# One score chunk of an attention kernel moved from ScalarE to VectorE, with joined norm exponentials and a new order of work

## The chip, the core and the metric

The kernel runs on one core of one Trainium2 chip. The metric is device time in microseconds (us), the median of several runs; smaller is better. Engines go by the profile's short names: PE is TensorE (matmuls), PEld its loading of weights, ACT is ScalarE, DVE is VectorE, POOL is GpSimd and SP the engine that issues most transfers.

## The reference

Attention on normalised vectors: 8 batches of 12 heads, 512 positions, 64 dimensions, tau = 0.1.

```python
def reference(Q, K, V, tau):                        # each (8, 12, 512, 64), float32
    Q_norm = Q / (norm(Q, axis=-1) + 1e-10)
    K_norm = K / (norm(K, axis=-1) + 1e-10)
    scores = einsum('bhqd,bhkd->bhqk', Q_norm, K_norm) / tau
    weights = exp(scores - max(scores))
    weights = weights / (sum(weights) + 1e-10)
    return einsum('bhqk,bhkd->bhqd', weights, V)
```

## The kernel before

Two heads of one batch make a pair; there are 48 pairs, 0 to 47. Every piece of work is an operation with a key, and the text speaks of it by that key: `SCO.24.1` is the score matmuls of pair 24, chunk 1. The operations of a pair s are:

- `LD.s.0`, `LD.s.1`, `LV.s` (SP): load Q, K and V of the pair, 256 KB each. Rings of 18 buffers for Q and K and 6 for V: `LV.s` waits until `VC.(s-6)` has read the buffer.
- `SQ.s` (POOL): squares of Q and K. `SSQ.s` (PE) and `RED.s` (DVE) sum them; `NEW.g.k` (DVE) are the Newton steps that turn the sums of a group g of up to two pairs into 1/norm. Steps 7 and, where one pair of the group is scaled on another engine than the other, 8, write the factors of K.
- `SCL.s.0` (DVE) and `SCL.s.1` (POOL, or DVE where the table `ON` says so): Q and K times 1/norm, as bf16.
- `TR.s` (PE) and `EVA.s` (DVE): transpose them and copy the transposes out of PSUM.
- `SCO.s.c` (PE), c from 0 to 3: a chunk of 128 keys against 512 queries for both heads, two matmuls into one of two halves of the score tile `sc_ps` (line 526). `EXP.s.c` (ACT, line 542): the exponential of 128x1024 scores, written as bf16 to `et`. The two halves alternate, so the SCO of a chunk waits for the EXP two chunks before it.
- `PV.s.h.t` (PE, line 570): `et` times V, with a column of ones that gives the sum of the weights; `RCP.s` and `NRM.s` (DVE) divide by it; `ST.s` (SP) stores. `et` has three buffers: `EXP.s` waits for the last PV of pair s-3.
- `VC.s` (POOL): V as bf16.

Pairs 0 to 2 (the head) take their 1/norm from ScalarE: `LN` and `EX` (line 286). There `EX.1.0` and `EX.1.1`, and `EX.2.0` and `EX.2.1`, are one for Q and one for K. Pair 0 is cut in halves by head (`LD.0.w.h`, `SQ.0.w.h`, `SCL.0.w.h`, `TR.0.w.h`, `EVA.0.w.h`, with w 0 for Q and 1 for K).

PSUM has a bank `n_ps` for the norms: sums, Newton steps and, in the head, factors lie in its first 272 columns. VectorE works in it with RED, NEW and SCL.

What sets the order: `ORDER` holds for each engine the list of its operations, written out by hand or by a planner outside of the file, and each engine does its list in that order. A wait of one operation holds back all that stands behind it on its engine. `schedule()` adds the waits for shared PSUM banks; `run()` turns every need into a semaphore.

A path for exponentials on VectorE is in the file but unused, since `SPLIT` is empty: `split()` (line 593) scores one head of a chunk into bank `x` (operation SCD), with a second matmul that adds a constant to lift the scores to the place where their bits are nearly those of a bf16 exponential, and four VectorE steps (EXD) then put a cubic correction on the low 16 bits and write the result as 16-bit integers.

The functions that the change touches, and what calls them:

## Time and profile before

| | before |
|---|---|
| median of 3 runs | 191.02 us |
| lowest and highest | 190.3 and 191.06 us |
| span of the profiled execution | 189.4 us |
| its own device time | not listed apart from the three |
| granted TensorE clock | 0.996 |
| exponentials of 128x1024 (line 542) | 184, 169.1 us busy |
| ScalarE busy | 181.7 us, 96% |
| TensorE, VectorE, GpSimd busy | 174.1, 148.1, 160.7 us |

The span runs from the first to the last instruction of one profiled execution; the device time has what lies around it as well. A busy time is the union of an engine's instructions, so where one starts before the one ahead of it has ended, the count times the mean is more than the busy time. In a row of the timeline stand the start, the duration, the engine, the line, what is written and read, and how many instructions were merged; in square brackets, the idle time of the engine before it and what ended that. A row of windows has the busy time of each engine in one stretch.

### The profile page before, as it was taken

What the parts mean: (1) busy time and instruction counts of PE and PEld (TensorE: products, weight loads), DVE (VectorE), ACT (ScalarE), POOL (GpSimd) and SP (SyncE); (2) the same over time, 40 slices, a digit from 0 to 9 for tenths busy, and PEclk for the clock granted to TensorE, in tenths of its full rate; (3) what the DMA queues carried; (4) which work ended last, traced back from release to release, by engine and by line L of the source; (5) the groups of instructions that cost most, each with busy time, mean ns of one, the idle gap of its engine ahead of it and who ended that gap; (6) DMA issues with size and microseconds to landing.
All of it is one profiled execution on the core that took longest, in us unless ns stands there. A gap on an engine that the chain in (4) does not pass through costs nothing.

```text
span 189.4 us, 7341 instructions
## 1 busy us (share of the span) xinstructions
PE 174.1 (92%) x3078; PEld 110.7 (58%) x3078; DVE 148.1 (78%) x453; ACT 181.7 (96%) x210; POOL 160.7 (85%) x147
## 2 busy tenths in 40 slices
...
GB/s 169 338 352 349 350 350 349 350 376 383 151 197 356 291 345 315 269 376 323 359 361 378 271 167 336 257 332 345 328 160 313 168 12 9 211 177 140 141 107 173
DMA packets 52448, 50.80 MB, mean 268 GB/s; under 512 B 3136, under 2 KB 52416, under 8 KB 52416
## 3 DMA queue, kind: packets, MB, share of 16 engines
...
q8 instruction: 24, 0.39, 0.9%
q10 hardware_dynamic: 432, 0.33, 0.6%
...
## 4 chain that ended last, share of the span: by engine, by line
ACT 82%; DVE 7%; PE 7%; DMA 1%; issue 1%
ACT et L542 80%; PE scps L526 2%; DMA qk<-in_Q_dram 1%; DVE qn L296 1%; PE bps L570 1%; DVE ob L586 1%; DVE qt L504 1%; ACT et L371 1%; PE bps L339 1%; PE bps L558 1%; DVE nps L276 1%; PE bps L268 1%; DVE ob L643 1%; PE bps L498 0%; DVE xs L324 0%
## 5 line engine op out<-in xcount | busy, mean ns | idle before, releaser
L542 ACT ACTIVATE et<-scps 128x1024 bf16<-128x1024 f32 x184 | 169.1, 1128 | 0.5 <-PE scps L526 0.4
L250 POOL TENSOR_TENSOR sq<-qk 128x1024 bf16<-128x1024 f32 (+2 forms) x48 | 87.9, 1848 | 5.1 <-DMA qk<-in_Q_dram 4.9
L526 PE MATMUL scps<-qt 64*128 64x512 bf16 x376 | 74.4, 385 | 8.4 <-ACT et L542 6.1
L570 PEld LDWEIGHTS bps<-vb,et 128*128 128x128 bf16 x1472 | 51.4, 98 | 24.1 <-issue 18.0
L570 PE MATMUL bps<-vb,et 128*128 128x65 bf16 x1472 | 65.1, 194 | 0.2
L296 POOL TENSOR_TENSOR qn<-qk,rk 128x512 bf16<-128x512 f32 x44 | 45.8, 1051 | 11.8 <-DVE rk L405 11.7
L504 DVE COPY qt<-bps 128x1024 bf16<-128x1024 bf16 x46 | 31.8, 691 | 10.1 <-PE bps L498 9.4
L296 DVE TENSOR_TENSOR qn<-qk,nps 128x512 bf16<-128x512 f32 (+1 forms) x51 | 33.9, 671 | 0.8 <-ACT nps L286 0.2
L586 DVE TENSOR_TENSOR ob<-bps,rd 128x512 f32<-128x512 f32 x47 | 32.5, 691 | 1.2
L526 PEld LDWEIGHTS scps<-qt 64*128 64x128 bf16 x376 | 18.2, 93 | 25.3 <-ACT et L542 13.4
L547 POOL TENSOR_SCALAR vb<-vf 128x512 bf16<-128x512 f32 x48 | 29.9, 634 | 0.0
L268 PE MATMUL bps<-sq,ident 128*128 128x128 bf16 x376 | 29.1, 220 | 0.0
L268 PEld LDWEIGHTS bps<-sq,ident 128*128 128x128 bf16 x376 | 21.2, 98 | 9.4 <-issue 6.3
L584 DVE RECIPROCAL rd<-bps 128x8 f32<-128x8 f32 x47 | 9.7, 207 | 17.7 <-PE bps L570 14.3
L498 PE MATMUL bps<-ident,qn 64*128 64x64 bf16 x736 | 18.8, 191 | 2.4 <-DVE ob L586 0.4
L498 PEld LDWEIGHTS bps<-ident,qn 64*128 64x128 bf16 x736 | 14.2, 95 | 9.8 <-DVE nps L276 4.0
L276 DVE TENSOR_REDUCE nps<-bps 128x16 f32<-128x128 f32 x45 | 13.4, 297 | 1.8 <-PE bps L268 1.8
L397 DVE TENSOR_TENSOR nps<-nps,ys 128x32 f32<-128x32 f32 (+1 forms) x48 | 9.2, 193 | 0.9
L401 DVE SCALAR_TENSOR_TENSOR nps<-nps,ys 128x32 f32<-128x32 f32 (+1 forms) x48 | 9.1, 191 | 0.8
L237 PE MATMUL scps<-warm_in 128*128 128x256 bf16 x22 | 4.8, 402 | 1.1 <-DVE warm_in L232 1.1
L409 DVE TENSOR_SCALAR ys<-nps 128x32 int32<-128x32 int32 (+1 forms) x24 | 4.4, 183 | 0.5
L405 DVE SCALAR_TENSOR_TENSOR nps<-nps,ys 128x16 f32<-128x16 f32 (+1 forms) x25 | 4.3, 175 | 0.3
...
## 6 DMA issues: line engine op xcount, KB each, us to landing
vf<-in_V_dram SPq DMA_DIRECT2D x48, 256.0 KB, 5.4
qk<-in_Q_dram SPq DMA_DIRECT2D x47, 256.0 KB, 5.9
qk<-in_K_dram SPq DMA_DIRECT2D x47, 256.0 KB, 5.7
out_dram<-ob SPq DMA_DIRECT2D x47, 256.0 KB, 4.4
...
```

The source lines that it names most:

```text
L250: emit = lambda e: e.tensor_tensor(out=b, in0=a, in1=a, op=ALU.mult)
L268: last = e.matmul(out=ps[:, 0:128], lhsT=ident[:, :], rhs=sq[s % R_SQ][:, :, 8 * k : 8 * k + 8], start=(k == 0), stop=(k == 7))
L276: lambda e: e.tensor_reduce(out=dst(None), in_=ps[:, 0:128].rearrange("p (w g e) -> p w g e", w=2, e=8), axis=AX.X, op=ALU.add))
L296: lambda e: e.tensor_tensor(out=o, in0=x, in1=r, op=ALU.mult))
L498: last = e.transpose(t_ps[:, k, b, :], qn[s % R_QN][ks, b // NT, b % NT].rearrange("p h d -> p (h d)"), ident[ks, ks])
L504: lambda e, lo=lo, hi=hi: e.tensor_copy(out=qt[iqt][:, :].rearrange("p w t (k x) -> p k (w t) x", k=2)[:, :, lo:hi], in_=t_ps[:, :, lo:hi]))
L526: last = e.matmul(out=sc_ps[:, 2 * b + k, :], lhsT=qt[iqt][64 * h : 64 * h + 64, 1, n, :], rhs=qt[iqt][64 * h : 64 * h + 64, 0, :, :], sta ...
L542: lambda e, c=c, b=b: e.activation(out=et[iet][:, c, :, :], in_=sc_ps[:, 2 * b : 2 * b + 2, :], func=ACT.Exp, scale=scale, bias=bias))
L547: lambda e: e.tensor_scalar(out=vb[:, iq, :, :, 0:DIM].rearrange("p c h d -> p h c d"), in0=vf[iv][:, :, :].rearrange("p h (c d) -> p h c ...
L570: last = e.matmul(out=o_ps[:, h, 65 * t : 65 * t + 65], lhsT=et[iet][:, c, h, 128 * t : 128 * t + 128], rhs=vb[:, iq, c, h, :], start=(c = ...
L584: lambda e: e.reciprocal(out=rd[io][:, :], in_=grid[:, :, :, DIM]))
L586: lambda e: e.tensor_tensor(out=ob[io][:, :], in0=grid[:, :, :, 0:DIM], in1=rd[io][:, :].unsqueeze(3).to_broadcast([128, 2, NT, DIM]), op= ...
```

## The change

- `SPLIT` names chunk 1 of pair 24. `SCO.24.1` and `EXP.24.1` go. For each head h and half j of the queries there is a `SCD.24.h.j` (PE: two matmuls of 256 columns) and four steps `EXD.24.h.j.0` to `.3` (DVE, 128x256). `split()` no longer scores 512 columns into bank `x` but 256 into the second half of the norm bank.
- Since PE then writes into a bank that VectorE uses all the time, `schedule()` makes each SCD wait for the last RED, NEW, SCL or EXD that stands on VectorE ahead of that SCD's first EXD. Each SCD also waits for the last EXD of the one before.
- The other three exponentials of pair 24 get the bias `SHIFT`, which makes them fit the shifted scale.
- For pairs 1 and 2 one EX does Q and K at once, so `EX.1.1` and `EX.2.1` go.
- `SCL.12.1` and `SCL.18.1` go from POOL to DVE; each splits a group's factors of K, so that `NEW.6.8` and `NEW.9.8` come in.
- Two memsets (`level0`, `level`) fill the constant's tile on DVE at the start.
- The order of all five engines is new. What else it moves that matters here: `LD.1.1` goes second on SP; `SQ.1.1.1` and `SQ.1.0` go ahead on ACT; `SQ.1.1.0` goes ahead of the EVA of pair 0 on DVE; `SSQ.1` goes ahead of the first score on PE; `SSQ.45` goes from ahead of `SCO.40.3` to behind it; V is converted (VC) earlier on POOL.

```diff
@@ -46,6 +46,12 @@
         by_token = {token(o.key): o for o in self.list}
         order = {e: [by_token.pop(t) for t in text.split()] for e, text in ORDER.items()}
         assert not by_token, list(by_token)[:8]
+        last = None
+        for o in order["dve"]:
+            if o.key[0] == "EXD" and o.key[-1] == 0:
+                self.ops[("SCD", *o.key[1:-1])].needs.append(last)
+            if o.key[0] in ("RED", "NEW", "SCL", "EXD"):
+                last = o.key
         for e, ops in order.items():
             before = {}
             for o in ops:
@@ -172,7 +178,8 @@
     t_ps = b_ps[:, 1:3, 0:256].bitcast(bf16).rearrange("p k (b x) -> p k b x", x=64)
     n_ps = nc.alloc_psum_tensor("nps", [128, 512], f32)
     spare = n_ps[:, 2 * W * (R_X + 2) : 2 * W * (R_X + 2) + 16 * LOGS]
-    y_u = x_ps[:, :].bitcast(u16).rearrange("p (x two) -> p x two", two=2)[:, :, 0]
+    y_ps = n_ps[:, 256:512]
+    y_u = y_ps.bitcast(u16).rearrange("p (x two) -> p x two", two=2)[:, :, 0]
 
     P = Program(nc)
     exd = []
@@ -459,13 +466,15 @@
             free = [("SCL", 0, 0, 1), ("SCL", 0, 1, 1)] if s == 1 else [("SCL", s - 1, 0)] + (
                 [k for k in (("SCL", s - 1, 1), ("SCL", s - 1, 1, 0), ("SCL", s - 1, 1, 1)) if k in P.ops]
                 if engine("pool", "SCL", s - 1, 1) == "dve" else [])
-            for w, dst in ((0, rq), (1, r)):
-                exps(s, (w,), dst, xl[s][:, w], ("LN", s), gain, free)
-            scaled(s, 0, "dve", rq, [("EX", s, 0), ("EX", s, 1)])
+            both = eng == "dve"
+            for w, dst in ((0, spare[:, 16 * s - 8 : 16 * s + 8]),) if both else ((0, rq), (1, r)):
+                exps(s, (w,), dst, xl[s][:, :, :].rearrange("p w x -> p (w x)") if both else xl[s][:, w], ("LN", s), gain, free)
+            done = [("EX", s, 0)] + ([] if both else [("EX", s, 1)])
+            scaled(s, 0, "dve", rq, done)
             for j in range(2) if s == 1 else ():
-                scaled(1, 1, eng, r, [("EX", 1, w) for w in range(2)], (j,), slice(2 * j, 2 * j + 2))
+                scaled(1, 1, eng, r, done, (j,), slice(2 * j, 2 * j + 2))
             if s > 1:
-                scaled(s, 1, eng, r, [("EX", s, w) for w in range(2)])
+                scaled(s, 1, eng, r, done)
         elif s:
             m, c8 = 8 * sizes[g], 8 * (s - first[g])
             x2 = x_slot(g).rearrange("p (w x) -> p w x", w=2)
@@ -561,7 +570,8 @@
                             start=(c == 0 and t == 0), stop=(c == NT - 1), skip_group_check=True)
                 return last
 
-            P.add(("PV", s, c), "pe", [("EXP", s, c), ("VC", s), ("PV", s, c - 1) if c else None], pv,
+            done = [("EXD", s, h, j, 3) for h in range(2) for j in range(2)] if SPLIT.get(s) == c else [("EXP", s, c)]
+            P.add(("PV", s, c), "pe", [*done, ("VC", s), ("PV", s, c - 1) if c else None], pv,
                   take=[] if c else ["o0", "o1"], until=("NRM", s))
         for h in range(2) if s not in CHUNKED else ():
             for t in range(NT):
@@ -593,28 +603,30 @@
     def split(s, c, ready, iqt, iet):
 
         for h in range(2):
-            hs = slice(64 * h, 64 * h + 64)
-
-            def scd(e, hs=hs):
-                e.matmul(out=x_ps[:, :], lhsT=level[hs, 0:128], rhs=level[hs, 128 : 128 + SEQ], start=True, stop=False)
-                return e.matmul(out=x_ps[:, :], lhsT=qt[iqt][hs, 1, c, :], rhs=qt[iqt][hs, 0, :, :], start=False, stop=True)
-
-            P.add(("SCD", s, h), "pe", ready + ["level"], scd, take=["x"], until=("EXD", s, h, 3))
-            w, done = wd[len(exd) % 2], exd[-2:-1]
-            steps = [
-                lambda e, w=w: e.tensor_scalar(
-                    out=w[:, :], in0=y_u, scalar1=1.0, scalar2=-65536.0, op0=ALU.mult, op1=ALU.add),
-                lambda e, w=w: e.tensor_tensor(out=w[:, :], in0=y_u, in1=w[:, :], op=ALU.mult),
-                lambda e, w=w: e.scalar_tensor_tensor(
-                    out=w[:, :], in0=y_u, scalar=65536.0 * CUBIC[1], in1=w[:, :], op0=ALU.add, op1=ALU.mult),
-                lambda e, w=w, h=h: e.scalar_tensor_tensor(
-                    out=et[iet][:, c, h, :].bitcast(u16), in0=w[:, :], scalar=128 * CUBIC[0] / 65536.0**3, in1=x_ps[:, :],
-                    op0=ALU.mult, op1=ALU.add)]
-            for k, step in enumerate(steps):
-                P.add(("EXD", s, h, k), "dve",
-                      [("EXD", s, h, k - 1) if k else ("SCD", s, h)] + (done if k == 0 else [])
-                      + ([key("PV", s - R_ET, 1, NT - 1)] if k == 3 else []), step)
-            exd.append(("EXD", s, h, 3))
+            for j in range(2):
+                hs, qs = slice(64 * h, 64 * h + 64), slice(256 * j, 256 * j + 256)
+
+                def scd(e, hs=hs, j=j):
+                    e.matmul(out=y_ps, lhsT=level[hs, 0:128], rhs=level[hs, 128:384], start=True, stop=False)
+                    return e.matmul(
+                        out=y_ps, lhsT=qt[iqt][hs, 1, c, :], rhs=qt[iqt][hs, 0, 2 * j : 2 * j + 2, :], start=False, stop=True)
+
+                P.add(("SCD", s, h, j), "pe", ready + ["level"] + exd[-1:], scd)
+                w = wd[len(exd) % 2][:, :]
+                steps = [
+                    lambda e, w=w: e.tensor_scalar(
+                        out=w, in0=y_u, scalar1=1.0, scalar2=-65536.0, op0=ALU.mult, op1=ALU.add),
+                    lambda e, w=w: e.tensor_tensor(out=w, in0=y_u, in1=w, op=ALU.mult),
+                    lambda e, w=w: e.scalar_tensor_tensor(
+                        out=w, in0=y_u, scalar=65536.0 * CUBIC[1], in1=w, op0=ALU.add, op1=ALU.mult),
+                    lambda e, w=w, h=h, qs=qs: e.scalar_tensor_tensor(
+                        out=et[iet][:, c, h, qs].bitcast(u16), in0=w, scalar=128 * CUBIC[0] / 65536.0**3, in1=y_ps,
+                        op0=ALU.mult, op1=ALU.add)]
+                for k, step in enumerate(steps):
+                    P.add(("EXD", s, h, j, k), "dve",
+                          [("EXD", s, h, j, k - 1) if k else ("SCD", s, h, j)]
+                          + ([key("PV", s - R_ET, 1, NT - 1)] if k == 3 else []), step)
+                exd.append(("EXD", s, h, j, 3))
 
     def final(s, iq, iet, io):
 
@@ final(), one of its needs @@
-                       scores_read(place[s, NT - 1] - 1) if i == 2 else None, ("VC", s),
+                       scores_read(place[s, NT - 1] - 1) if i == 2 else None, ("VC", s), *exd,
@@ -671,8 +683,8 @@
 TINY = 1e-19
 WARM = 19
 FILL = (3, 0)
-ON = {'SQ.0.0.1': 'pool', 'SCL.2.1': 'dve', 'SCL.3.1': 'dve', 'LD.1.1': 'sp', 'SCL.1.1': 'dve'}
-SPLIT = {}
+ON = {'SQ.0.0.1': 'pool', 'SCL.2.1': 'dve', 'SCL.3.1': 'dve', 'LD.1.1': 'sp', 'SCL.1.1': 'dve', 'SCL.12.1': 'dve', 'SCL.18.1': 'dve'}
+SPLIT = {24: 1}
 BINADE = 144
 SHIFT = 11.78350206951907
 CUBIC = (0.07826797, 3.89144693)
```

Of the orders, the places that the prediction speaks of (- before, + after):

```diff
ORDER["sp"], the first loads
-        LD.0.0.0 LD.0.0.1 LD.1.0 LD.1.1 LD.2.0 LD.2.1 LD.3.0 LD.3.1 LD.4.1 LV.0 LD.4.0 LD.5.0 LD.5.1 LV.1 LD.6.1
+        LD.0.0.0 LD.1.1 LD.0.0.1 LD.1.0 LD.2.1 LD.2.0 LD.3.1 LD.3.0 LV.0 LD.4.1 LD.4.0 LD.5.1 LD.5.0 LD.6.0
...
ORDER["pool"], the start
-        SQ.0.0.1 one eye vone SQ.2.0 SQ.2.1 SQ.3.0 VC.0 SQ.4.0 SQ.5.0 VC.1 SQ.6.0 SQ.7.0 SCL.4.1 VC.2 SQ.9.0 SCL.5.1
+        one eye vone SQ.0.0.1 SQ.2.1 SQ.2.0 SQ.3.0 VC.0 SQ.4.0 SQ.5.0 VC.1 SQ.6.0 VC.2 SQ.7.0 SCL.4.1 VC.3
...
ORDER["dve"], the start, and pairs 21 to 24
-        wz RED.0.0.0 RED.0.1.0 RED.0.1.1 SCL.0.0.0 SCL.0.1.0 RED.0.0.1 EVA.0.0.0 EVA.0.1.0 SCL.0.0.1 SQ.1.1.0
+        wz level0 level RED.0.0.0 RED.0.1.0 RED.0.1.1 SCL.0.1.0 SCL.0.0.0 SQ.1.1.0 RED.0.0.1 EVA.0.1.0 EVA.0.0.0
+        SCL.0.0.1 SCL.0.1.1 RED.1.0 EVA.0.0.1 EVA.0.1.1 SCL.1.1.0 SCL.1.0 SCL.1.1.1 RED.2.0 EVA.1.0 EVA.1.1.0
...
+        SCL.25.0 RCP.20 NRM.20 RED.27.0 NEW.13.0 NEW.13.1 NEW.13.2 EVA.24 EXD.24.0.0.0 NEW.13.3 EXD.24.0.0.1
+        NEW.13.4 RCP.21 EXD.24.0.0.2 NEW.13.5 EXD.24.0.0.3 NRM.21 EXD.24.0.1.0 NEW.13.7 RED.28.0 EXD.24.0.1.1
+        NEW.13.6 EXD.24.0.1.2 EXD.24.0.1.3 EVA.25 EXD.24.1.0.0 SCL.26.0 EXD.24.1.0.1 RCP.22 EXD.24.1.0.2
+        EXD.24.1.0.3 RED.29.0 NRM.22 EXD.24.1.1.0 NEW.14.0 EVA.26 NEW.14.1 NEW.14.2 SCL.27.0 RCP.23 NEW.14.3
+        NRM.23 NEW.14.4 EXD.24.1.1.1 NEW.14.5 EVA.27 EXD.24.1.1.2 NEW.14.7 EXD.24.1.1.3 NEW.14.6 RED.30.0
+        SCL.28.0 RCP.24 NRM.24 RED.31.0 NEW.15.0 NEW.15.1 NEW.15.2 EVA.28 NEW.15.3 NEW.15.4 SCL.29.0 NEW.15.5
...
ORDER["pe"], the head, and pairs 21 to 24
-        warm.0 warm.1 warm.2 warm.3 warm.4 warm.5 warm.6 warm.7 warm.8 warm.9 warm.10 warm.11 warm.12 warm.13 warm.14
-        warm.15 warm.16 warm.17 warm.18 TR.0.0.0 TR.0.1.0 fill.0 fill.1 fill.2 SCO.0.0.0 SCO.0.0.1 TR.0.0.1 SSQ.1
...
+        warm.0 warm.1 warm.2 warm.3 warm.4 warm.5 warm.6 warm.7 warm.8 warm.9 warm.10 warm.11 warm.12 warm.13
+        warm.14 warm.15 warm.16 warm.17 warm.18 TR.0.1.0 TR.0.0.0 fill.0 fill.1 fill.2 SSQ.1 SCO.0.0.0 SCO.0.0.1
+        TR.0.0.1 TR.0.1.1 SCO.0.0.2 SCO.0.0.3 SCO.0.1.0 SCO.0.1.1 SSQ.2 TR.1.1.0 TR.1.0 SCO.0.1.2 SCO.0.1.3
...
+        SSQ.27 SCO.22.2 TR.24 PV.21.0.0 SCO.22.3 PV.21.0.1 PV.21.0.2 SCD.24.0.0 SCO.23.0 PV.21.0.3 PV.21.1.0
+        PV.21.1.1 PV.21.1.2 PV.21.1.3 SCO.23.1 SSQ.28 SCO.23.2 SCD.24.0.1 SCO.23.3 PV.22.0.0 TR.25 SCO.24.0
+        PV.22.0.1 PV.22.0.2 PV.22.0.3 SCO.24.2 SCD.24.1.0 SCO.24.3 PV.22.1.0 PV.22.1.1 PV.22.1.2 PV.22.1.3
+        SCO.25.0 SSQ.29 SCO.25.1 SCD.24.1.1 SCO.25.2 TR.26 PV.23.0.0 PV.23.0.1 PV.23.0.2 SCO.25.3 PV.23.0.3
+        PV.23.1.0 PV.23.1.1 PV.23.1.2 PV.23.1.3 SCO.26.0 SCO.26.1 TR.27 PV.24.0.0 SCO.26.2 PV.24.0.1 PV.24.0.2
+        PV.24.0.3 SSQ.30 SCO.26.3 PV.24.1.0 PV.24.1.1 PV.24.1.2 PV.24.1.3 SCO.27.0 SSQ.31 SCO.27.1 PV.25.0.0
+        TR.28 SCO.27.2 PV.25.0.1 PV.25.0.2 SCO.27.3 PV.25.0.3 PV.25.1.0 PV.25.1.1 PV.25.1.2 PV.25.1.3 SCO.28.0
...
ORDER["pe"], pair 40
-        PV.38.1.0 PV.38.1.1 PV.38.1.2 PV.38.1.3 SSQ.45 SCO.40.3 SCO.41.0 TR.42 PV.39.0.0 PV.39.0.1 PV.39.0.2 SCO.41.1
+        PV.38.1.1 SCO.40.2 PV.38.1.2 PV.38.1.3 SCO.40.3 SSQ.45 SCO.41.0 TR.42 PV.39.0.0 PV.39.0.1 SCO.41.1
...
ORDER["act"], the head
-        LD.0.1.0 LD.0.1.1 table SQ.0.0.0 SQ.0.1.0 SQ.0.1.1 LN.0.0 EX.0.0 LN.0.1 EX.0.1 SQ.1.0 SQ.1.1.1 EXP.0.0.0
-        EXP.0.0.1 LN.1 EX.1.1 EX.1.0 EXP.0.0.2 EXP.0.1.0 LN.2 EX.2.1 EX.2.0 EXP.0.1.1 EXP.1.0 EXP.1.1 EXP.1.2 EXP.1.3
+        LD.0.1.0 LD.0.1.1 table SQ.0.0.0 SQ.0.1.0 SQ.0.1.1 SQ.1.1.1 LN.0.0 EX.0.0 SQ.1.0 LN.0.1 EX.0.1 EXP.0.0.0
+        LN.1 EXP.0.0.1 EX.1.0 EXP.0.0.2 EXP.0.1.0 LN.2 EX.2.0 EXP.0.1.1 EXP.1.0 EXP.1.1 EXP.1.2 EXP.1.3 EXP.2.0
...
```

260 lines of the change are left out of this document (127 added, 133 removed).

## The prediction

> **What bounds the kernel now.** I read the page's busy shares first, then its chain, then the chain in order of time.
>
> ```profile
> span 189.4 us, 7341 instructions
> PE 174.1 (92%) x3078; PEld 110.7 (58%) x3078; DVE 148.1 (78%) x453; ACT 181.7 (96%) x210; POOL 160.7 (85%) x147
> ...
> ACT 82%; DVE 7%; PE 7%; DMA 1%; issue 1%
> ...
> L542 ACT ACTIVATE et<-scps 128x1024 bf16<-128x1024 f32 x184 | 169.1, 1128 | 0.5 <-PE scps L526 0.4
> ```
>
> ```profile
> 28.00 0.32 PE scps L526
> 28.32 0.32 issue
> 28.64 0.40 PE scps L526
> 29.04 0.02 issue
> 29.06 130.32 ACT et L542 x142
> 159.38 0.02 issue
> 159.41 22.11 ACT et L542 x24
> ```
>
> ScalarE is 96% busy and carries 82% of the chain. From 29.06 to 181.52 us the chain is nothing but exponentials: 142 in 130.32 us, 0.918 us each. One lasts 1.128 us, but the next starts before it ends, so a removed one is worth 0.918 and not 1.128. Before 29.06 the chain passes through VectorE and TensorE. At 28.32 TensorE stands still for 0.32 us inside a pair of score matmuls with no releaser, and at 159.38 an exponential starts only when its predecessor has ended: there ScalarE was short of scores, and lost the 1.128 - 0.918 = 0.21 us of overlap at least.
>
> The three times of before (median 191.02, lowest 190.3) lie 0.9 to 1.7 us above the span; the profiled execution's own time is not listed. I work against the span of 189.4 and add 1.6, the median less the span.
>
> **Chunk 1 of pair 24.** ScalarE loses one exponential: -0.92 us, as long as scores reach it on time for its whole run. TensorE loses one SCO and gains four SCD (two matmuls of 256 columns each); VectorE gains sixteen EXD steps of 128x256. No row shows an EXD. The nearest, with those of the work around it:
>
> ```profile
> L296 DVE TENSOR_TENSOR qn<-qk,nps 128x256 bf16<-128x256 f32 x2 | 0.8, 417 | 0.1
> L643 DVE TENSOR_TENSOR ob<-nps,rd 128x256 f32<-128x256 f32 x1 | 0.4, 425 | 0.0
> L296 DVE TENSOR_TENSOR qn<-qk,nps 128x512 bf16<-128x512 f32 x49 | 33.2, 681 | 0.6 <-ACT nps L286 0.2
> L586 DVE TENSOR_TENSOR ob<-bps,rd 128x512 f32<-128x512 f32 x47 | 32.5, 691 | 1.2
> L504 DVE COPY qt<-bps 128x1024 bf16<-128x1024 bf16 x46 | 31.8, 691 | 10.1 <-PE bps L498 9.4
> L276 DVE TENSOR_REDUCE nps<-bps 128x16 f32<-128x128 f32 x45 | 13.4, 297 | 1.8 <-PE bps L268 1.8
> L584 DVE RECIPROCAL rd<-bps 128x8 f32<-128x8 f32 x47 | 9.7, 207 | 17.7 <-PE bps L570 14.3
> L397 DVE TENSOR_TENSOR nps<-nps,ys 128x32 f32<-128x32 f32 x42 | 8.2, 195 | 0.9
> L526 PE MATMUL scps<-qt 64*128 64x512 bf16 x376 | 74.4, 385 | 8.4 <-ACT et L542 6.1
> ```
>
> I take 0.42 per EXD, from the two 128x256 rows that read the norm bank; the ends are 0.30 (the reduction of 128 columns) and 0.69 (twice the columns). 16 x 0.42 = 6.7 us. In the new order VectorE has, from the end of EVA.24 to EXD.24.1.1.3, also 3 RCP, 3 NRM, 12 NEW, 2 RED, 3 EVA and 2 SCL: 0.62 + 2.07 + 2.34 + 0.59 + 2.07 + 1.36 = 9.1 us. Together 15.8 us by durations.
>
> What room is there?
>
> ```profile
> 92.00:106.80 14.80, 13.87 (x268) 8.97 (x267) 11.56 (x36) 14.80 (x17) 14.75 (x13) 1.00 1.06 356
> ```
>
> (Columns: TensorE, weight loads, VectorE, ScalarE, GpSimd.) In these four pairs VectorE is idle for 3.2 us and TensorE for 0.9. The result is needed when PV.24.1.0 stands at the head of TensorE's queue, just after SCO.26.3. SCO.22.2 goes out at the end of exponential 22.0, TR.24 behind it takes 0.4, EVA.24 0.69: EVA.24 ends about 0.7 us into exponential 22.2. SCO.26.3 goes out when 26.1 ends. Between lie 22.2 to 26.1 without 24.1, 15 exponentials: 15 x 0.918 - 0.7 + 0.4 = 13.5 us, and some 0.8 later PV.24 would still be done before SCO.27.0 must be: 14.3 us. By durations VectorE is 1.5 us too late. But its instructions overlap too:
>
> ```profile
> 90.24 0.17 DVE L405 SCALAR_TENSOR_TENSOR rk<-nps,ys 128x16 f32<-128x16 f32 x1
> 90.33 0.17 DVE L405 SCALAR_TENSOR_TENSOR nps<-nps,ys 128x16 f32<-128x16 f32 x1
> ...
> 91.15 0.69 DVE L504 COPY qt<-bps 128x1024 bf16<-128x1024 bf16 x1
> ...
> 91.75 0.68 DVE L296 TENSOR_TENSOR qn<-qk,nps 128x512 bf16<-128x512 f32 x1
> ```
>
> One starts 0.08 to 0.09 before the one ahead ends, unless it reads its result. The new order puts a NEW, RCP, NRM, EVA or SCL between most EXD steps, so about 30 of the 41 instructions overlap: -2.5 us, 13.3 us. The added waits: each SCD waits for VectorE's last user of the norm bank ahead of its EXD, and EXD step 0 waits for SCD. A turn is two matmuls, 0.35 us by the 0.385 row, and 0.05 of signals. The first is bare, since nothing stands between EVA.24 and EXD.24.0.0.0: +0.4. NRM.21, EVA.25 and NRM.22 (0.69 each) cover the other three. Sum 13.7 of 14.3 us: it fits by 0.6. On TensorE SCO.23.0, 23.3, 24.3 and 25.2 are queued behind the four SCD, and ScalarE waits for them. The tightest is SCD.24.1.1, which waits for EXD.24.1.0.3 and RED.29: walking both queues with these durations, it goes out about 8.75 us after exponential 22.2 starts, 0.4 us before SCO.25.2 could start anyway. TensorE gains 4 x 0.35 - 0.39 = 1.0 us in the stretch, and only three TR and three SSQ fall in it where four pairs have four, which gives it back. With margins of 0.1 to 0.6 us I charge +0.3, between 0 and +2.
>
> [...]
>
> **The joined norm exponentials, and the head.**
>
> ```profile
> 0.79 0.86 SPq L321 DMA_DIRECT2D qk<-in_Q_dram  x2
> 1.70 0.43 SPq L436 DMA_DIRECT2D qk<-in_Q_dram  x1
> 2.16 0.47 SPq L436 DMA_DIRECT2D qk<-in_K_dram  x1
> 3.48 1.20 ACT L248 ACTIVATE sq<-qk 128x256 bf16<-128x256 f32 x3 [0.50 <-DMA qk<-in_Q_dram]
> 4.12 0.61 POOL L250 TENSOR_TENSOR sq<-qk 128x256 bf16<-128x256 f32 x1 [3.63 <-DMA qk<-in_Q_dram]
> 4.71 0.21 ACT L282 ACTIVATE xl<-xs 128x8 f32<-128x8 f32 x1
> 7.31 2.41 POOL L250 TENSOR_TENSOR sq<-qk 128x512 bf16<-128x512 f32 x2 [1.26 <-DMA qk<-in_Q_dram]
> 7.41 0.41 DVE L250 TENSOR_TENSOR sq<-qk 128x256 bf16<-128x256 f32 x1
> 7.64 1.08 ACT L371 ACTIVATE et<-scps 128x512 bf16<-128x512 f32 x2
> 9.07 0.22 ACT L282 ACTIVATE xl<-xs 128x16 f32<-128x16 f32 x1 [0.35 <-DVE xs L276]
> 9.32 0.28 ACT L286 ACTIVATE nps<-xl 128x8 f32<-128x8 f32 x2
> 9.62 1.94 ACT L371 ACTIVATE et<-scps 128x1024 bf16<-128x1024 f32 x2
> ...
> 12.81 7.41 ACT L542 ACTIVATE et<-scps 128x1024 bf16<-128x1024 f32 x8
> ...
> 3.40:9.70 6.30, 5.97 (x42) 3.39 (x40) 5.29 (x15) 4.43 (x15) 4.18 (x6) 1.00 1.01 326
> ```
>
> Two EX take 0.28 where one takes 0.18 (0.173 mean): -0.10 for EX.2.1; EX.1.1 lies in the head's sum. In the head SQ.1.1.1 now stands ahead of LN.0.0 on ScalarE and needs LD.1.1, which goes second on SP, ahead of LD.0.0.1. When does LD.1.1 land? LD.0.0.1 in that place fed GpSimd at 4.12; 128 KB more at 326 GB/s is 0.4: 4.5. From the other end, LD.2.0 fed GpSimd at 7.31 with 1280 KB moved; LD.1.1 closes 640 KB, 2.0 us less: 5.3. I take 5.0, nearer to the second, which has the sharing of several transfers in it. Then SQ.1.1.1 (0.41) ends at 5.41 and LN.0.0 starts at 5.44 and not 4.71: +0.73. VectorE's SQ.1.1.0 (0.41, 0.33 with overlap) moves ahead of both EVA that the first score needs: the first exponential at 7.64 + 0.73 + 0.33 = 8.7. LN.1 and one EX follow without the idle 0.35: EXP.0.0.0, LN.1, EXP.0.0.1, EX.1.0 make some 1.4 where before 1.98 passed to 9.62. ScalarE is full from 10.1 and not 9.62: +0.45, between -0.3 (no wait for the load, and the 0.35 gone) and +1.2 (LD.1.1 at 5.8).
>
> **The new orders.** From 12.81 to 29.06 ScalarE started 17 exponentials in 16.25 us, 0.65 over 17 x 0.918. I put 0.35 of it to TensorE's stop at 28.32 and 0.3 to late norms and squares, since the chain runs through VectorE there. GpSimd starts its squares as before, so a later ScalarE absorbs those: -0.3. At 159.38 SSQ.45 stood ahead of the late SCO.40.3; now it stands behind: -0.2. TensorE's 0.32 at 28.32 I leave as it is.
>
> Two K products on VectorE: +2 x (0.68 + 0.17 for a NEW), covered by VectorE's idle time ahead of RCP (17.7 us); without it they would delay EVA of pairs 12 and 18. GpSimd loses 2 x 1.05 us (its SCL has 45.8 us x44). The memsets of level lie in VectorE's idle time before the first RED. On SP stores and loads change places throughout: the waits of ST.1, LV.7, LD.23.1 and LV.16 hold up what is queued behind them.
>
> ```profile
> qk<-in_Q_dram SPq DMA_DIRECT2D x47, 256.0 KB, 5.9
> ```
>
> A load lands 5.9 us after its issue, so SP is several transfers ahead, and a wait of a few us only uses that up. If LD.33.0, behind LV.38 (which waits for VC.32), came late, SQ.33 on GpSimd would be next, four pairs ahead of its TR. All at 0.
>
> **Sum:** -0.92 - 0.10 + 0.30 + 0.45 - 0.30 - 0.20 = -0.77: span 188.6, time 190.2. A change of 0.5%, 0.95 us, is about what a measurement of this kernel can tell from none.
>
> **Rivals.**
> 1. Everything meets: the head costs nothing, the stretch nothing, and the 0.32 goes too: -0.92 - 0.10 - 0.30 - 0.20 - 0.32 = -1.84, 189.2. For it: ScalarE's saturation from 29.06. Against: SQ.1.1.1 must wait for a load.
> 2. VectorE's instructions do not overlap around EXD: 16.2 us in 14.3, 1.9 late, 1.6 over my 0.3: 191.8. The four starts above speak against it.
> 3. VectorE becomes the bound (slower): an EXD, three of four of which read every second 16-bit word of the norm bank, takes 0.6 or more. Each 0.1 adds 1.6 us: 16 x (d - 0.42) - 0.6 late, in place of my 0.3. From d = 0.46 it is late, from 0.52 the change is as slow as before, from 0.58 slower by 0.95. At 0.62 it is 2.6 late, 192.5; at 0.69, 3.7 and 193.6. For it: no row has this access. Against: no 128x256 row is above 0.43.
> 4. The load of pair 1's K lands at 5.8: 190.2 + 0.75 = 191.0, no change. For it: seven transfers share the engines there, and the last packets of one can lag; against: both estimates end by 5.3.
>
> **How the numbers follow.** My forecast 0.52 (its own range 189.7 to 190.7; 0.20 of it below 190.07), rival 1 0.20, rival 2 0.05, rival 3 0.08, rival 4 0.15. Faster 0.20 + 0.20 = 0.40; slower (over 191.97) all of rival 3, half of 2 and 0.02 of 4: 0.13; within 0.47. The range 189.2 to 191.7 leaves out rival 3, half of 2 and half of 1: 0.2.
>
> **What would show it.** 183 exponentials of pairs 1 to 46 in place of 184; sixteen VectorE rows of 128x256 near 0.42; ScalarE's first 128x1024 exponential near 10.1; no ScalarE idle between pairs 22 and 27. ScalarE waiting there for SCO.25.2, or TensorE for EXD, would make it wrong; so would EXD rows above 0.46, or the first LN after 6.

## The result, and the profile after

The change made the kernel slower: 206.8 us (203.44 to 207.87) against 190.97 (190.3 to 191.06), a ratio of 1.072, 95% interval 1.064 to 1.080. Ratios and intervals, here and below, leave out executions more than 1.5% above the fastest of the same kernel (of the four here, 207.52 and 207.87), so the ratio speaks of 13.7 us where the medians differ by 15.8. The prediction had 190.2 and a range to 191.7. The profiled execution took 206.07 us. The lines of its page that answer to those of before:

```profile
span 204.2 us, 7355 instructions
PE 180.2 (88%) x3084; PEld 113.7 (56%) x3084; DVE 154.4 (76%) x475; ACT 183.1 (90%) x207; POOL 158.5 (78%) x145
...
POOL 32%; ACT 18%; DVE 14%; PE 13%; DMA 12%; issue 6%; SPq 4%; ACTq 0%; POOLq 0%; DVEq 0%
...
L551 ACT ACTIVATE et<-scps 128x1024 bf16<-128x1024 f32 x183 | 171.0, 1049 | 12.1 <-PE scps L535 11.6
```

ScalarE has one exponential fewer, but its share of the chain fell from 82% to 18%: it is no longer the bound. It stood 11.6 us for scores (before 0.4), and GpSimd leads the chain. GpSimd's waits, from the waits of the changed kernel and then of the kernel before (total, count, longest):

```profile
POOL sq L257 <- DMA qk<-in_Q_dram: 8.1, 4, 4.0
POOL vb L556 <- DMA vf<-in_V_dram: 6.5, 6, 2.1
POOL sq L257 <- DMA qk<-in_K_dram: 3.3, 3, 1.6
```

```profile
POOL sq L250 <- DMA qk<-in_Q_dram: 4.9, 2, 3.6
POOL sq L250 <- DMA qk<-in_K_dram: 0.2, 1, 0.2
```

Before, GpSimd waited for loads only in the head; after, eleven times behind it as well. One case from end to end, from the timeline of the changed kernel (SP's queue, GpSimd, TensorE, ScalarE):

```profile
73.88 1.41 SPq L443 DMA_DIRECT2D qk<-in_K_dram  x1
78.27 0.37 SPq L446 DMA_DIRECT2D vf<-in_V_dram  x1
...
82.20 0.98 SPq L443 DMA_DIRECT2D qk<-in_Q_dram  x2
83.22 0.47 SPq L443 DMA_DIRECT2D qk<-in_K_dram  x1
...
89.15 1.89 POOL L257 TENSOR_TENSOR sq<-qk 128x1024 bf16<-128x1024 f32 x1 [1.58 <-DMA qk<-in_K_dram]
...
91.10 0.62 PE L275 MATMUL bps<-sq,ident 128*128 128x128 bf16 x8 [1.45 <-POOL sq L257]
91.65 0.61 PE L535 MATMUL scps<-qt 64*128 64x512 bf16 x4
...
92.08 1.94 ACT L551 ACTIVATE et<-scps 128x1024 bf16<-128x1024 f32 x2 [1.70 <-PE scps L535]
```

SP stands from 75.29 to 78.27 in front of LV.24, whose buffer is taken. LD.38.0, for a pair 13 ahead of LD.25.1, goes out before it. LD.25.1 goes out at 83.22 and lands at 89.08, so SQ.25 starts 1.58 us late. TensorE's list has SSQ.25 right ahead of SCO.20.2, a score of the pair in hand: TensorE stands 1.45 us, and ScalarE 1.70. The load named in the prediction went the same way: LD.33.0 landed at 118.97, GpSimd had waited 2.11 us, TensorE 0.66 for SSQ.33, ScalarE 0.46 in front of EXP.28.1.

The largest single loss comes late. EXP.47.0 starts 14.3 us later than in the run sorted by need (below), and 5.7 of them are lost behind EXP.41.0. LV.47 lands at 165.85; its conversion VC.47 stands in GpSimd's list ahead of SCL.42.1, the K product that the transpose of pair 42 needs:

```profile
165.93 1.21 POOL L556 TENSOR_SCALAR vb<-vf 128x512 bf16<-128x512 f32 x2 [2.12 <-DMA vf<-in_V_dram]
...
170.97 0.56 PE L507 MATMUL bps<-ident,qn 64*128 64x64 bf16 x16 [2.01 <-POOL qn L303]
...
172.66 1.02 ACT L551 ACTIVATE et<-scps 128x1024 bf16<-128x1024 f32 x1 [2.35 <-PE scps L535]
```

Starts in us of the first exponential of a pair, as the traces have them ("control" and "by need" are runs below):

```
               before   after  control  by need  no split  old orders + split
EXP.1.0         12.81   14.29    12.38    12.71     12.60     12.19
EXP.6.0         31.79   32.88    30.83    31.63     30.96     31.23
EXP.20.0        83.09   88.43    82.24    83.81     83.16     82.63
EXP.24.0        97.59  106.50    96.73    98.58     97.98     99.12
EXP.25.0       101.20  109.21   100.35   101.29    101.59    101.83
EXP.28.0       112.36  120.49   111.50   112.84    113.27    112.98
EXP.47.0       182.25  197.25   181.39   182.94    184.24    183.18
```

### The profile page after: what moved, and what is told of

Its sections match the earlier page's. It is cut to its first block, busy times and chain, and to the rows that moved or that the text cites. A ratio compares the mean times of both kernels' runs of the same rounds, so it can differ in the third digit from the quotient of the medians.

```text
span 204.2 us, 7355 instructions
## 1 busy us (share of the span) xinstructions
PE 180.2 (88%) x3084; PEld 113.7 (56%) x3084; DVE 154.4 (76%) x475; ACT 183.1 (90%) x207; POOL 158.5 (78%) x145
## 4 chain that ended last, share of the span: by engine, by line
POOL 32%; ACT 18%; DVE 14%; PE 13%; DMA 12%; issue 6%; SPq 4%; ACTq 0%; POOLq 0%; DVEq 0%
POOL sq L257 17%; ACT et L551 16%; POOL qn L303 7%; POOL vb L556 7%; DMA qk<-in_K_dram 5%; DMA vf<-in_V_dram 5%; PE scps L535 4%; PE bps L580 3%; DVE qn L303 3%; SPq L443 3%; DVE qt L513 2%; DMA out_dram<-ob 2%; DVE ob L596 2%; PE bps L275 2%; DVE nps L283 1%
## 5 line engine op out<-in xcount | busy, mean ns | idle before, releaser
L551 ACT ACTIVATE et<-scps 128x1024 bf16<-128x1024 f32 x183 | 171.0, 1049 | 12.1 <-PE scps L535 11.6
L580 PE MATMUL bps<-vb,et 128*128 128x65 bf16 x1472 | 70.1, 198 | 0.4 <-DVE qt L513 0.2
L580 PEld LDWEIGHTS bps<-vb,et 128*128 128x128 bf16 x1472 | 54.1, 100 | 27.1 <-issue 16.9
L303 POOL TENSOR_TENSOR qn<-qk,rk 128x512 bf16<-128x512 f32 x42 | 43.5, 1043 | 10.1 <-DVE rk L412 9.5
L303 DVE TENSOR_TENSOR qn<-qk,nps 128x512 bf16<-128x512 f32 (+1 forms) x53 | 35.0, 669 | 0.3 <-ACT nps L293 0.2
L507 PE MATMUL bps<-ident,qn 64*128 64x64 bf16 x736 | 19.3, 194 | 7.7 <-POOL qn L303 2.4
L507 PEld LDWEIGHTS bps<-ident,qn 64*128 64x128 bf16 x736 | 14.3, 96 | 16.1 <-issue 6.9
L378 ACT ACTIVATE et<-scps 128x1024 bf16<-128x1024 f32 (+1 forms) x5 | 4.1, 847 | 2.1 <-PE scps L373 2.1
L244 PE MATMUL scps<-warm_in 128*128 128x256 bf16 x22 | 4.2, 368 | 1.1 <-DVE warm_in L239 1.1
```

Source lines behind the costliest of these rows:

```text
L303: lambda e: e.tensor_tensor(out=o, in0=x, in1=r, op=ALU.mult))
L507: last = e.transpose(t_ps[:, k, b, :], qn[s % R_QN][ks, b // NT, b % NT].rearrange("p h d -> p (h d)"), ident[ks, ks])
L551: lambda e, c=c, b=b: e.activation(out=et[iet][:, c, :, :], in_=sc_ps[:, 2 * b : 2 * b + 2, :], func=ACT.Exp, scale=scale, bias=bias))
L580: last = e.matmul(out=o_ps[:, h, 65 * t : 65 * t + 65], lhsT=et[iet][:, c, h, 128 * t : 128 * t + 128], rhs=vb[:, iq, c, h, :], start=(c = ...
```

## The experiments

Theories: (A) SP's new order starves GpSimd; (B) the EXD and SCD of pair 24 overload VectorE and TensorE; (C) GpSimd's new order is itself at fault. The kernel before, run beside each of them, took 190.98 to 191.38 us.

**Which list.** Four runs. First, SP's list alone, sorted: a load is needed when GpSimd's list, walked with the durations of its rows, comes to it; among the entries whose buffer is free, the one needed first goes next.

```diff
 the changed kernel, ORDER["sp"] alone (the first 13 entries stay)
-... LD.6.1 LD.8.0 LV.2 LD.7.0 LV.7 LD.9.0 LD.9.1 LV.3 ...
+... LD.6.1 LV.2 LD.7.1 LD.7.0 LV.3 LD.9.0 LD.9.1 LD.8.0 LD.8.1 LV.4 LV.7 ...
-... LV.24 ST.13 LD.35.1 LD.34.1 LD.35.0 LD.26.1 LD.28.0 LD.38.0 LD.25.1 ...
+... LD.24.0 LD.24.1 LD.25.0 LD.25.1 LV.20 LV.18 ST.10 LD.26.0 ...
```

> The changed kernel with one list new: SP's. Its 193 transfers are put in the order in which GpSimd's list needs the loads (each load once its buffer is free, each store within four pairs of its NRM); the lists of the other four engines are untouched. Theory A (SP's order: loads that GpSimd needs soon stand behind loads for pairs far ahead and behind waits): GpSimd's 18 us of waiting for loads fall below 4, ScalarE's 11.6 us of waiting for scores below 2, time 190 to 193. Theory B (the sixteen EXD and four SCD overload VectorE and TensorE): the time stays above 203. Theory C (GpSimd's order, with the V conversions far ahead): stays above 200, with GpSimd still waiting.

Measured: 193.0 us (191.71 to 193.93), ratio 1.007 (1.002 to 1.012). Its page and its waits:

```profile
span 189.9 us, 7353 instructions
...
ACT 46%; POOL 17%; DVE 16%; PE 14%; issue 3%; DMA 2%; ACTq 0%; DVEq 0%
```

```profile
ACT et L551 <- PE scps L535: 0.5, 2, 0.4
```

By the ratios (1.072 and 1.007) some 12 of the 14 us are gone, with the split chunk and all other new lists in place. The mirror puts the suspected lists into the kernel before:

```diff
 the kernel before
-ORDER["sp"], ORDER["pool"] of before
+ORDER["sp"], ORDER["pool"] of the change; SCL.12.1, SCL.18.1 (with NEW.6.8, NEW.9.8) on DVE
```

> The mirror: the kernel before with SP's and GpSimd's lists of the changed one (SCL.12.1 and SCL.18.1 on VectorE right behind SCL.12.0 and SCL.18.0, since they are not in that GpSimd list). No split chunk, no joined EX, VectorE, TensorE and ScalarE in their old order. A or C: most of the 15 us come with the two lists, 202 to 208, with GpSimd waiting for loads 12 us or more. B: 190.5 to 192.5.

Measured: 206.28, 209.91, 209.98 and 210.31 us, with no EXD in it. In the trace, of the execution of 209.91, ScalarE starves as in the change:

```profile
ACT et L542 <- PE scps L526: 15.8, 22, 3.2
```

Two more, the first the run by need with `SPLIT` empty, the second the changed kernel with both old lists:

```diff
 the run by need
-SPLIT = {24: 1}
+SPLIT = {}          (SCO.24.1 and EXP.24.1 back, SCD and EXD out of the lists)
```

> e1 without the split chunk: EXP.24.1 and SCO.24.1 are back, SCD, EXD and the two memsets are gone, everything else as in e1. It prices the split alone, with the loads in order. By the prediction's term the split is worth -0.92 + 0.3: e3 is 0.6 us slower than e1 (0 to 0.9). B: e3 is over 2 us faster than e1.

Measured: 194.03 us (192.76 to 195.63, and one execution of 335.52), 1.0 slower than with the split chunk (ratios to before 1.011 to 1.020 and 1.002 to 1.012). So B falls: in these lists the chunk costs nothing, and by the medians gains.

```diff
 the changed kernel
-ORDER["sp"], ORDER["pool"] of the change
+ORDER["sp"], ORDER["pool"] of before, without SCL.12.1 and SCL.18.1
```

> The changed kernel with SP's and GpSimd's lists of before (less SCL.12.1 and SCL.18.1, which VectorE has). The three other engines keep the new lists, which were not made for these two, so some waits of GpSimd on VectorE may come in. A or C: 190 to 195. B: above 203.

Measured: 195.61, 196.93 and 198.53 us, a ratio of 1.028 (1.014 to 1.042), and one execution of 740 us (below). The profile is of that one, so where the others lost can't be read.

**What in SP's order.** Two halves: entries that wait for a buffer, and loads for far pairs in front of near ones.

```diff
 the changed kernel, ORDER["sp"] alone
+ an entry whose buffer isn't free steps back behind those that can go (LV.7 by 7 places, LV.24 by 15)
```

> The changed kernel with its own order of SyncE, except that an entry whose buffer is not yet free when its turn comes steps back behind the entries that can go (64 of 193 entries move by two places or more; LV.7 seven places, LV.24 fifteen, LD.38.0 seventeen). The loads for pairs far ahead stay early. The list by need ran at 193.0 us, the changed kernel at 206.8. If the waits of SyncE (about 3 to 5 us each, ten of them) leave the queue empty and that carries the loss: 193 to 196. If the loss is that loads for pairs far ahead take the transfers' turns ahead of the near ones: 200 to 206, with GpSimd still waiting for LD.12.0, LD.15.0, LD.25.1 near 43, 48 and 89 us.

```diff
 the changed kernel, ORDER["sp"] alone
+ the 38 loads that landed over 20 us ahead of their use are issued 14 us ahead of it
```

> The mirror of the run without waits: the changed kernel with the 38 loads that landed over 20 us before their use issued 14 us before it, all other entries in their order, so that entries that find their buffer taken (LV.7, ST.5, LV.16, LV.20, LV.24, LV.38, LV.46) still hold up what stands behind them. If the turns given to far loads carry the loss: 193 to 196. If the waits do: 200 to 206, with SyncE's gaps before LV.7, LV.24, LV.42, LV.43 as long as before. If both carry about half: 196 to 200 in both runs.

Measured: 200.1 (199.6 to 200.34) and 201.71 us (200.28 to 204.67), ratios of 1.046 and 1.052. Against 1.072 each half gives back some 4 to 5 us, and the whole sorted list 12; neither half alone does it. The trace by stretches (the last column is GB/s, the one before it the DMA engines' share; ScalarE's busy time is the fourth), of the kernel before, the changed one, and the run without waits:

```profile
20.00:40.00 20.00, 18.62 (x351) 11.86 (x348) 16.32 (x51) 19.52 (x22) 19.26 (x18) 1.00 1.10 352
40.00:60.00 20.00, 18.85 (x349) 12.01 (x346) 17.25 (x55) 20.00 (x23) 20.00 (x18) 1.00 0.85 282
```

```profile
20.00:40.00 20.00, 19.07 (x356) 11.89 (x353) 17.12 (x55) 19.90 (x22) 18.52 (x18) 1.00 0.99 328
40.00:60.00 20.00, 17.71 (x306) 11.40 (x304) 16.41 (x53) 18.65 (x21) 18.01 (x15) 1.00 0.96 315
```

```profile
60.00:80.00 20.00, 17.18 (x289) 10.87 (x288) 14.75 (x44) 17.25 (x19) 17.24 (x17) 0.91 1.09 373
```

From 40 to 60 us the changed kernel moves more than the one before and yet starves; without waits, from 60 to 80 us, the transfers run at 373 GB/s and ScalarE is still idle for 2.75 of 20 us. So it is not the amount moved. Nor does the count of waits or of far loads tell: SP's gaps of over 1 us up to 125 us sum to 25.7 us before and 27.1 after, ten gaps in each, and the control (below), as fast as before, has 52 loads over 20 us early against 38. What goes with the loss is how many of the 140 loads that GpSimd reads (pairs 0 and 1 aside, but for their V) land less than 0.2 us ahead of GpSimd's use: 2 before, 2 in the control, 7 by need, 11 without waits, 16 after. Behind the head GpSimd waits for loads 0 us before and in the control, 1.6 by need, 9.0 without waits, 12.9 after.

**A control, and one wait by itself.**

```diff
 the kernel before
-ORDER["sp"] of before
+ORDER["sp"] sorted by the need of before's GpSimd list
```

> A control: the kernel before with only SyncE's list sorted by GpSimd's need, by the same rule as in the run of 193.0 us. If the rule is as good as the list before: 191 (190.3 to 191.6), and what the run of 193.0 us still lost came from the other lists. If the rule itself costs something: 192 to 193.5, and then the changed lists of the other engines cost nothing.

Measured: 190.79 us, ratio 0.998 (0.995 to 1.001): the rule costs nothing, and the 2 us or so up to 193.0 come with what else the change brings.

```diff
 the control
-... LD.7.0 LD.7.1 LV.2 ... ST.1 LV.7 LV.8 ...
+... LD.7.0 LD.7.1 LV.7 LV.2 ... ST.1 LV.8 ...
```

> The control (the kernel before, SyncE's list by need, 190.8 us) with one entry moved: LV.7 from behind ST.1 to right behind LD.7.1, where the changed kernel has it. LV.7 must wait for VC.1, which ends at 16.79 us, and the entry in front of it is issued at 10.1, so SyncE stands for about 5.5 us and the transfers run dry from about 17.5 to 20 us. If a wait at the head of SyncE's list is paid by GpSimd: LD.9.1 lands 2 to 3 us later, past SQ.9.0's start at 22.04, and the time is 192 to 193.5. If a wait of a few us only uses up SyncE's lead, as the prediction had it: 190.8.

Measured: 191.06 us, no difference. SP stood 5.7 us and the nearest load came late:

```profile
10.25 0.95 SPq L436 DMA_DIRECT2D qk<-in_K_dram  x1
16.93 0.88 SPq L439 DMA_DIRECT2D vf<-in_V_dram  x2
...
23.11 1.89 POOL L250 TENSOR_TENSOR sq<-qk 128x1024 bf16<-128x1024 f32 x1 [0.91 <-DMA qk<-in_K_dram]
```

SQ.9 started 1.07 us later than in the control and EXP.47.0 0.67: of 5.7 us, lead paid 5. One wait was nearly free here, where the loads behind it had lead. That several waits and the far loads together use the lead up is the reading of these runs; none prices them one by one.

**GpSimd's list.**

```diff
 the changed kernel
-ORDER["pool"] of the change
+ORDER["pool"] of before without SCL.12.1, SCL.18.1; ORDER["sp"] by its need
```

> The changed kernel with the GpSimd list of before (less SCL.12.1 and SCL.18.1, which stay on VectorE) and SyncE's list sorted by the need of that list; ScalarE, VectorE and TensorE as changed. If GpSimd's new order costs the 1.5 to 2 us by which the run by need (193.0) stands behind the kernel before: 191.0 or below. If GpSimd's order is worth nothing: 193.0. If the other engines' lists were made for the new order of GpSimd, late K products hold up transposes: 194 to 198.

Measured: 193.36 us: under the new lists of the others either GpSimd list does. The other way round:

```diff
 the run by need
+ORDER["pe"], ORDER["dve"], ORDER["act"] of before outside the pairs 21 to 27
```

> The run by need (193.0 us) with the orders of before on TensorE, VectorE and ScalarE outside the pairs 21 to 27: GpSimd's list, SyncE's list by need, the split chunk and the two K products on VectorE stay as changed. If the remaining 2 us lie in the new orders of TensorE, VectorE and ScalarE (starts of EXP.6.0, EXP.16.0 and EXP.21.0 each 0.4 to 0.6 us later than in the control): 190.5 to 191.2. If they lie in GpSimd's new order or the K products: 193. If GpSimd's new order fits only the new orders of the others: above 193.

Measured: 201.69 us. GpSimd's new list under the others' old ones holds up TensorE (its waits):

```profile
PE bps L507 <- POOL qn L303: 4.9, 5, 1.3
...
PE bps L275 <- POOL sq L257: 3.3, 5, 1.3
```

So C holds only as a mismatch of lists: what the old lists of TensorE ask for next, products and squares, comes later in GpSimd's new one. With that, much of the mirror's loss of 15 to 19 us is this mismatch and not SP's order: here GpSimd waits 2.3 us for loads behind the head, and some 10 us are lost all the same.

**The sums as the deadline.**

```diff
 the changed kernel, ORDER["pe"]
-SSQ.12 SCO.9.2 TR.10 PV.8.0.0 SCO.9.3
+SCO.9.2 TR.10 PV.8.0.0 SCO.9.3 SSQ.12      (likewise SSQ.25 behind SCO.21.0, SSQ.33 behind SCO.28.2; their RED later)
```

> The changed kernel with SyncE's and GpSimd's lists as they are; only three sums move: SSQ.12 from ahead of SCO.9.2 to behind SCO.9.3, SSQ.25 from ahead of SCO.20.2 to behind SCO.21.0, SSQ.33 from ahead of SCO.28.1 to behind SCO.28.2, with RED.12, RED.25 and RED.33 (and the Newton steps behind the first two) behind EVA.10, EVA.22 and EVA.29 on VectorE. In the changed kernel's trace LD.25.1 lands at 89.08, SQ.25.0 starts 1.58 us late, SSQ.25 holds TensorE for 1.45 and ScalarE stands 1.70 us before EXP.20.2; 0.48 before EXP.9.2 and 0.46 before EXP.28.1 in the same way. If a late load reaches ScalarE because TensorE's list is in order and the sum stands ahead of the next scores: those three idle times go, 206.8 - 2.6 = 204. If GpSimd's lateness is what counts whatever the place of the sum: the idle times come back within two pairs, before the transposes, and the time stays at 206 to 207.

Measured: 205.02 us (202.49 to 206.53), which overlaps the changed kernel's 203.44 to 207.87. In the trace all three idle times go. Around pair 25, EXP.20.0 to EXP.22.0 takes 9.46 in place of 10.72 us. But 0.48 is back at EXP.28.3, and in front of EXP.9.3 and EXP.10.0 more comes than went:

```profile
45.89 0.41 PE L507 MATMUL bps<-ident,qn 64*128 64x64 bf16 x16 [1.21 <-POOL qn L303]
...
47.16 1.02 ACT L551 ACTIVATE et<-scps 128x1024 bf16<-128x1024 f32 x1 [1.09 <-PE scps L535]
49.79 1.02 ACT L551 ACTIVATE et<-scps 128x1024 bf16<-128x1024 f32 x1 [1.60 <-PE scps L535]
```

The sum's place decides where a late square is paid first; GpSimd's lateness then comes back as a late K product, unless it has lead.

**The split chunk under the orders of before.** Three placements of the stretch, and the two products, all with SP by need:

```diff
 the control with SPLIT = {24: 1}, joined EX
+ORDER["dve"] from RED.27.0 to NRM.24, ORDER["pe"] of pairs 22 to 24 of the change; SCD.24.0.1 behind SSQ.28
```

> The change without its new orders: the orders of before (SyncE's sorted by need, as in the control at 190.8 us) with the split chunk of pair 24, the joined norm exponentials and both K products back on GpSimd; only VectorE's entries from RED.27.0 to NRM.24 and TensorE's of pairs 22 to 24 are the changed kernel's. By the terms of the prediction that the runs have borne out so far (EXP.24.1 gone 0.92, second norm exponential gone 0.10, VectorE and TensorE crowded 0.30) 190.8 - 0.7 = 190.1, a ratio to before of 0.993 to 0.997. If the new orders of the pairs 5 to 21 cost nothing and the split itself is what keeps the run by need at 193.0: 192 to 193. If VectorE's sixteen rows hold up transposes under the old order: 191 to 192.

Measured: 194.79 us (193.88 to 195.04). The place I gave SCD.24.0.1 cost it: TensorE stood for EXD.24.0.0.3, and ScalarE 2.43 us.

```profile
98.12 0.28 PE L610 MATMUL nps<-level 64*128 64x256 bf16 x1 [1.16 <-DVE et L622]
...
100.00 2.85 ACT L551 ACTIVATE et<-scps 128x1024 bf16<-128x1024 f32 x3 [2.43 <-PE scps L535]
```

```diff
 the run above
+SCL.12.1, SCL.18.1 (NEW.6.8, NEW.9.8) on DVE
```

> The run beside it (before's orders, split chunk, joined exponentials) with SCL.12.1 and SCL.18.1 moved from GpSimd to VectorE as in the change. The prediction put the two products at nothing, since GpSimd has its work ahead of its use. If so: the same as the run beside it within 0.4 us. If VectorE has no room at pairs 12 and 18: 0.3 to 1 us more. If GpSimd was late somewhere behind pair 12: up to 0.5 us less.

Measured: 195.5 us; in the trace 0.43 at pair 11 and nothing at 18.

```diff
 the run before the last
+the stretch longer: ORDER["pe"] from SCO.20.3 to PV.26.1.3, ORDER["dve"] from EVA.20 to EVA.29 of the change
```

> The run that put the split chunk into the orders of before lost 2.4 us before EXP.24.0, where TensorE stood behind SCD.24.0.1 (placed behind SSQ.28 by hand) until EXD.24.0.0.3 was done, and 1.2 before EXP.27.0. Here the stretch is taken from the changed kernel as a whole: TensorE from behind SCO.20.3 to PV.26.1.3, VectorE from behind EVA.20 to EVA.29; all else is before's, SyncE by need. By the intervals between the starts of EXP.20.0 and EXP.28.0 (29.26 us in the control, 29.03 in the run by need) and the norm exponential: 190.8 - 0.3 = 190.5, and 190.1 if the 0.92 less 0.30 of the prediction holds in full. If the split chunk can't be had without the new orders of the other pairs: over 191.5.

Measured: 191.97 us, ratio 1.005 (1.003 to 1.006). EXP.24.0 to 25.0 is 0.91 us shorter than in the control, and 1.6 us were lost where the stretch begins. Mending that place (SCO.21.0 to SCO.21.2 earlier) and its end

```diff
-SSQ.25 TR.22 PV.19.0.0 PV.19.0.1 PV.19.0.2 SCO.21.0 ...
+SSQ.25 SCO.21.0 TR.22 PV.19.0.0 PV.19.0.1 SCO.21.1 ...
```

> The split chunk in the orders of before (191.97 us) lost 1.6 us before EXP.21.0, where the changed kernel's list begins with TR.22 ahead of SCO.21.0 and PV.19 waits for NRM.18, and 0.3 before EXP.29.0, where it ends; the interval from EXP.24.0 to EXP.25.0 is 0.9 shorter than in the control. Here two places of TensorE's list are mended: SCO.21.0, SCO.21.1, SCO.21.2 go ahead of TR.22 and of PV.19's later products, and SCO.29.0 ahead of SSQ.32. If the split chunk is worth its 0.9 less the crowding of 0.3 to 0.4: 190.2 to 190.5, against 190.8 of the control and 191.0 of the kernel before. If the crowding moves on to the next place where TensorE stands for VectorE: 191 to 192 again, and the split chunk gives nothing without an order planned as a whole.

gave 192.16 us: the wait moved on to EXP.22.0. The stretch needs TensorE about a chunk ahead, and under the old orders that lead costs more than the chunk gives. No version was measurably faster than the kernel before; the fastest was the control.

**The head.**

```diff
 the run by need
+the head of before on all engines (SP's first four loads; ACT to EXP.1.0, PE to TR.0.1.1, DVE to EVA.1.1.0, SQ.0.0.1 first on POOL)
```

> The run by need (193.0 us; starts of EXP.0.0.2 and EXP.1.0 in its trace 9.57 and 12.71) with the head of before on all engines: SyncE's first four loads, GpSimd's SQ.0.0.1 first, ScalarE's list to EXP.1.0, TensorE's to TR.0.1.1, VectorE's to EVA.1.1.0 (the joined exponentials stay). In the traces of eight kernels with LD.1.1 second, LD.0.0.1 lands between 4.86 and 6.05 and EXP.1.0 starts between 12.6 and 14.9; in the kernel before 4.04 and 12.81, in the control 12.38. The prediction charged the head 0.45. If the head's spread is what keeps the run by need behind: 191.7 to 192.2, with a narrower spread of its times than 191.7 to 193.9. If the head costs nothing: 193.0 again, and the rest lies in the orders of TensorE and VectorE in the pairs 5 to 21.

Measured: 192.7 us (192.07 to 194.11): the old head does not bring the run by need up to the control. It is no clean test, for in its trace EXP.1.0 starts at 13.45, with 0.53 us of waiting for scores, against 12.71 by need and 12.38 in the control. Behind the head both traces fall behind the control at the same places: 0.4 us at pair 15, 0.4 from 18 to 21. What is left there are the new orders of TensorE and VectorE; which entries of them cost it stays open.

## Why the prediction was wrong, step by step

**SP's order, put at 0, was the step that failed.** "A load lands 5.9 us after its issue, so SP is several transfers ahead, and a wait of a few us only uses that up" holds for one wait (0.67 us of 5.7 reached the end). It was never added up over the list: in the changed kernel 13 loads come when GpSimd already waits, 11 of them behind the head. Nor was it asked whether a near load stands behind far ones. And "SQ.33 on GpSimd would be next, four pairs ahead of its TR" named the wrong deadline: SSQ.33 stands in TensorE's list right ahead of SCO.28.1. VC.47 shows a second way that the prediction did not have: a late load of V holds up a K product. Sorting this one list takes 206.8 to 193.0.

**The exponential, -0.92:** right; EXP.24.0 to EXP.25.0 takes 2.71 us after and by need, 3.62 in the control.

**EXD at 0.42:** right, and rivals 2 and 3 fall. From the end of EVA.24 to the end of EXD.24.1.1.3 it takes 13.6 us (forecast 13.7), and 32 of the 41 instructions start 0.06 to 0.09 us before the one ahead has ended (forecast about 30). From the groups of VectorE by shape:

```profile
L622 DVE SCALAR_TENSOR_TENSOR et<-wd,nps 128x256 uint16<-128x256 f32 x4 | 1.7, 420 | 0.1
L617 DVE TENSOR_SCALAR wd<-nps 128x256 f32<-128x256 uint16 x4 | 1.7, 420 | 0.5 <-PE scps L535 0.5
L619 DVE TENSOR_TENSOR wd<-nps,wd 128x256 f32<-128x256 uint16 x4 | 1.7, 417 | 0.0
L620 DVE SCALAR_TENSOR_TENSOR wd<-nps,wd 128x256 f32<-128x256 uint16 x4 | 1.6, 408 | 0.0
```

**Crowding, +0.30:** by this measure mis-sized. EXP.20.0 to 28.0 takes 29.03 us by need and 29.26 in the control, 0.23 less and not 0.91, which leaves 0.68; under the old orders it was 2.0 (30.35 us). But the control has other lists: in the same lists without the chunk the stretch takes 30.11, so how much of the 0.68 is the chunk's and how much the new orders' isn't shown.

**The head, +0.45:** LD.1.1 landed at 4.99 (forecast 5.0) and LN.0.0 began at 5.46 (5.44). Behind that the sum fails: ScalarE was full from 11.19, +1.57.

```profile
4.83 0.72 ACT L255 ACTIVATE sq<-qk 128x256 bf16<-128x256 f32 x2 [0.98 <-DMA qk<-in_K_dram]
5.46 0.19 ACT L289 ACTIVATE xl<-xs 128x8 f32<-128x8 f32 x1
...
6.89 0.63 ACT L255 ACTIVATE sq<-qk 128x512 bf16<-128x512 f32 x1 [1.02 <-DMA qk<-in_Q_dram]
...
7.57 1.04 PE L275 MATMUL bps<-sq,ident 128*128 128x128 bf16 x8
...
8.54 1.03 PE L373 MATMUL scps<-qt 64*128 64x512 bf16 x2
...
9.18 0.60 ACT L378 ACTIVATE et<-scps 128x512 bf16<-128x512 f32 x1 [1.35 <-PE scps L373]
...
11.19 1.94 ACT L378 ACTIVATE et<-scps 128x1024 bf16<-128x1024 f32 x2 [0.74 <-PE scps L373]
```

Two things were left out. The loads that LD.1.1 passes land later, LD.1.0 at 6.87 and not 5.90: SQ.1.0 waits for it, and SSQ.1, which now stands ahead of the first score, waits for SQ.1.0. And TensorE was granted a clock of 0.50 from 7.24 to 10.65: SSQ.1 took 1.04 us and the two matmuls of the first score 1.03, against 0.61 and 0.60 by need, where the clock was full. So the head isn't steady: with the same head by need EXP.0.0.2 started at 9.57, where LD.1.0 landed at 6.13.

The first square that waits above reads a load that ScalarE issues itself, at 1.23 us and before at 1.22; it landed at 4.81 and before at 4.25. Of the loads issued by then only the order on SP differs: at 1.23 us SP issued LD.1.1 (256 KB) where before it issued LD.0.0.1 (128 KB). So in these two traces a new order on SP's queue went with a landing 0.56 us later on ScalarE's.

**Joined EX, -0.10:** right, 0.19 us for one (0.28 for two before). **SSQ.45, -0.20:** right, EXP.40.0 to 41.0 takes 3.80 us by need and 4.05 before. **Late norms, -0.30:** can't be told; EXP.1.0 to 6.0 takes 18.59 us in the changed kernel, 18.92 by need and 18.98 before, but 18.45 in the control, which has before's lists but for SP's. **K products at 0:** 0.4 us under the old orders.
